# A fixed emission order and ordering edges for the expert stage of a one-core hybrid encoder layer

## The chip, the cores and the metric

One core of one Trainium2 chip runs the whole layer. The metric is the device time of one execution in microseconds (us); before the change the median of three runs is 1244.87 us.

## What is computed

One layer over 1024 tokens of width 1024: a combined projection, differential attention and a state-space mixer, an output projection with LayerNorm that gives `h`, and a mixture of 32 experts on `h`, with a closing LayerNorm. The change touches the experts alone. The reference picks one of four groups for each token and two of its eight experts, and then computes, for each expert `e` and the tokens that chose it:

```python
def block_fn(args):
    tok, w, e = args
    xb = h2d[tok]
    hid = jax.nn.silu(xb @ w_gate[e]) * (xb @ w_up[e])
    yb = hid @ w_down[e]
    return yb * w[:, None].astype(yb.dtype)
```

`w_gate` and `w_up` are 1024 x 512 and `w_down` is 512 x 1024 per expert, all in float32. A first block of 128 places per expert is worked off in straight code; tokens beyond 128 of one expert go to a loop at the end, which these inputs leave empty.

## The kernel before

Attention, the mixer, the output projection and the routing come first and are not changed. The experts start about 540 us into the span and end near 1190 us; a tail adds the two results of each token and normalizes.

**Weights.** Each expert has six pieces of 1 MB: two halves each of gate (`g0`, `g1`), up (`u0`, `u1`) and down (`d0`, `d1`). SyncE's queue (SP) loads a piece into a ring of 12 buffers (`load_next`, L1169 and L1173; three more buffers at the start). `split_next` then writes it as a high and a low part, so that three fast matmul passes stand for a full-precision one: ScalarE (ACT) rounds to the high part (`split`, L172), VectorE (DVE) subtracts for the low part (L153), each in two instructions a piece. There are three pairs of split buffers (`NSPL = 3`): the split of piece n+3 writes where piece n was, and so waits for the product of piece n.

**Products.** `product` issues 12 matmuls of 128x512 for a piece (L1235 for gate and up, L1226 for down). The list `order` names the pieces: `g0 u0 g1 u1` of expert e, then `d0 d1` of expert e-1.

**Turning.** `tokens(e)` transposes the 128 gathered rows of an expert (eight matmuls against the identity into `xT`, L1199) and splits them into `xe`. `hidden(e)` applies silu to the gate sum (ACT, L1205, into `hd`, which the trace calls `gx`), multiplies by the up sum (DVE, L156), transposes that (four matmuls into `hT`, L1209) and splits it into `he`. `result(e)` scales the down sum (ACT, `yo`, L1242), adds the residual (DVE, L162), scatters the rows and gathers those of expert e+5 (POOL, L1139 and L1134).

**Overflow table.** Where piece 63, the second down half of expert 9, is to be loaded, `overflow_blocks` first uses its buffer for 25 small DVE instructions on the routing (tiles `over`, `place`, `blk`, `meta`), with one matmul (`counts`). The load of that piece waits for the last reader of that buffer. SP, like the other engines, also reads `meta` into a register for the loop at the end (L1340), and that read stands in SP's queue among the loads.

**What sets the order.** The program's text does not set the order on an engine. The framework traces the program and schedules it at build time by its own estimate of times; whatever is estimated to be ready first is put first. The result is one fixed list per engine, and on the chip each engine works its list off in order.

Of the kernel before, what the change touches and what calls it, by code (L numbers as in the profile page):

```python
# [11 lines left out]
F32 = mybir.dt.float32  # L12
F32R = mybir.dt.float32r
BF16 = mybir.dt.bfloat16
I32 = mybir.dt.int32
AF = mybir.ActivationFunctionType
# [3 lines left out]
P = 128  # L20
D = 1024
# [5 lines left out]
NE = 32  # L27
# [3 lines left out]
EPS = 1e-5  # L31
NSLOT = 25
NONE = 4096
STATS, MULS, ADDS, NGRP = 'VVVVVAVV', 'QQGGGVGQ', 'VVVVVVVV', 1
GB = 0
ASK, GLU, WO = (6, 12), (15, 16, 1, 20, 21, 1), (22, 24, 26, 30)
# [7 lines left out]
NEARSPL = 0  # L44
# [68 lines left out]
def tile_kernel(ctx: ExitStack, tc: tile.TileContext, I: dict, out: bass.AP, dbg=None):  # L113
    nc = tc.nc
    V, S, G, PE, SP = nc.vector, nc.scalar, nc.gpsimd, nc.tensor, nc.sync
# [7 lines left out]
    sl = Slots()  # L123
# [19 lines left out]
    h_dram = dram.tile([T, D], F32, name="h_dram")  # L143
# [11 lines left out]
    def mul(out_, a, b, eng=V):  # L155
        eng.tensor_tensor(out=out_, in0=a, in1=b, op=ALU.mult)  # L156
# [951 lines left out]
    NRAW, NSPL, NXG = 12, 3, 5  # L1108
# [11 lines left out]
    def gx(e):  # L1120
        return gxs[e % NXG // 2][:, e % NXG % 2, :]

    def deep(n):

        if NSPL <= n < NSPL + NLENT:
            return lent[n - NSPL], NRAW + NLENT
        return raw_ring[(n if n < NSPL else n - NLENT) % NRAW], NRAW + (NLENT if n < NRAW + NSPL + NLENT else 0)
# [3 lines left out]
            G.memset(gx(j), 0.0)  # L1131

    def gather(dst, ix):
        G.indirect_dma_start(out=dst, out_offset=None, in_=h_dram[:, :],  # L1134
                             in_offset=bass.IndirectOffsetOnAxis(ap=ix, axis=0),
                             bounds_check=T - 1, oob_is_err=False)

# [20 lines left out]
    def load_next():  # L1158
        n = st_["load"]
        if n == NOVER:  # L1160
            over.extend(overflow_blocks(deep(n)[0]))
        e, m = order[n]
        j = int(m[1])
        slot = deep(n)[0]
        if m[0] == "d":
            r = sl.at(slot, [P, 2, D], F32, f"rw{e}{m}")
            src = w_d[e, 256 * j:256 * j + 256, :].rearrange("(p k) n -> p k n", p=P)
            for ks in (slice(0, 1), slice(1, 2)) if n == len(order) - 1 else (slice(0, 2),):
                SP.dma_start(r[:, ks, :], src[:, ks, :])  # L1169
        else:  # L1170
            r = sl.at(slot, [P, 4, 512], F32, f"rw{e}{m}")
            src = w_g if m[0] == "g" else w_u
            SP.dma_start(r, src[e, 512 * j:512 * j + 512, :].rearrange("(p k) n -> p k n", p=P))  # L1173
        raws[e, m] = r
        st_["load"] += 1

    def split_next():
        n = st_["split"]
        e, m = order[n]
        r = raws.pop((e, m))  # L1180
        a, b = (sl.at(spl_ring[2 * (n % NSPL) + j], list(r.shape), F32R, f"w{'hl'[j]}{e}{m}") for j in range(2))
        if n == len(order) - 1:
            for j in range(2):
                for hs in HALVES:
                    split(a[:, j, hs], b[:, j, hs], r[:, j, hs])
        else:
            n = r.shape[1] // 2
            for j in range(2):
                js = slice(j * n, j * n + n)
                split(a[:, js, :], b[:, js, :], r[:, js, :])  # L1190
        hls[e, m] = (a, b)
        st_["split"] += 1

    def tokens(e):

        g_ = gx(e)
        b_ = bank2(f"xT{e}")
        for kt in range(KT):
            PE.transpose(b_[:, kt * P:(kt + 1) * P], rows(g_, kt), ident)  # L1199
        xT[e] = t_ = xes[e % 2]  # L1200
        split(t_[:, 0], t_[:, 1], b_.rearrange("p (k q) -> p k q", k=KT))

    def hidden(e):
        g_, u_ = acc.pop((e, "g")), acc.pop((e, "u"))
        S.activation(hd[:, 0, :], g_, AF.Silu)  # L1205
        mul(hd[:, 1, :], u_, hd[:, 0, :])
        b_ = bank(f"hT{e}", 1)
        for kt in range(4):
            PE.transpose(b_[:, kt * P:(kt + 1) * P], places(hd[:, 1, :], kt), ident)  # L1209
        t_ = hes[e % 2]  # L1210
        split(t_[:, 0], t_[:, 1], b_.rearrange("p (k q) -> p k q", k=4))
        hid[e] = t_

    def product(e, m):
        a, b = hls.pop((e, m))
        j = int(m[1])
        if m[0] == "d":
            if j == 0:
                acc[e, "y"] = bank2(f"y{e}")
            y = acc[e, "y"]  # L1220
            for k in range(2):
                kt = 2 * j + k
                passes = list(enumerate(((0, a), (0, b), (1, a))))
                for hs, (n, (x_, w_)) in ([(hs, p_) for hs in HALVES for p_ in passes] if e == NE - 1 else
                                          [(hs, p_) for p_ in passes for hs in HALVES]):
                    PE.matmul(y[:, hs], hid[e][:, x_, kt, :], w_[:, k, hs],  # L1226
                              start=(kt == 0 and n == 0), stop=(kt == 3 and n == 2))
        else:
            if j == 0:
                acc[e, m[0]] = bank(f"{m[0]}{e}")  # L1230
            o = acc[e, m[0]]
            for k in range(4):
                kt = 4 * j + k
                for n, (x_, w_) in enumerate(((0, a), (0, b), (1, a))):
                    PE.matmul(o, xT[e][:, x_, kt, :], w_[:, k, :],  # L1235
                              start=(kt == 0 and n == 0), stop=(kt == KT - 1 and n == 2))
# [14 lines left out]
    def overflow_blocks(key):  # L1251
# [45 lines left out]
        op.close()  # L1297
        return meta, place, blk

    for e in (0, 1, 4):  # L1300
        gather(gx(e), idx[:, 0, e:e + 1])
    tokens(0)
    for n, (e, m) in enumerate(order):
        while st_["split"] < min(len(order), n + NSPL):
            while st_["load"] < min(len(order), st_["split"] + deep(st_["load"])[1]):
                load_next()
            k = st_["split"]
            with ExitStack() as late_:
                if k < NSPL:
                    late_.enter_context(tc.issue_after((normed if k < NEARSPL else routed).ins))  # L1310
                    if k > 0:
                        late_.enter_context(tc.issue_after(turned.ins))
                split_next()
        if n == NLENT:
            he_all = sl.at(lent[0], [P, 2, 2, 4, P], F32R, "he")
            hes = [he_all[:, j] for j in range(2)]
            gxs[1] = sl.at(lent[1], [P, 2, D], F32, "gx1")
            yos = sl.at(lent[2], [P, 2, D], F32, "yo")
            for j in (2, 3):
                G.memset(gx(j), 0.0)  # L1320
                gather(gx(j), idx[:, 0, j:j + 1])
        product(e, m)
        if m == "u1":
            hidden(e)
        if m == "g1" and e + 1 < NE:
            tokens(e + 1)
        if m == "d1":
            result(e)
    meta, place, blk = over
    sl.back([deep(n)[0] for n in range(len(order) - NRAW, len(order))])  # L1330

# [149 lines left out]
```

## Time and profile before

| | |
|---|---|
| runs | 1244.34, 1244.87, 1251.14 us (median 1244.87) |
| profiled execution | 1243.16 us, of which the span of the trace is 1241.4 us |
| PE (matmul) busy | 1101.2 us (89%) |
| DVE busy | 970.2 us (78%) |
| ACT busy | 703.2 us (57%) |
| DMA bytes, mean rate | 271.01 MB, 218 GB/s |
| mean granted clock of TensorE | 0.934 |

The span runs from the first to the last instruction; the 1.8 us around it belong to the execution and not to any engine. A share is a mean over stages with different limits, and the stage in question is about half of the span. PE's clock has two levels, 1.2 and 2.4 GHz; the profile gives it as a share of the higher (0.5 and 1.00).

### The profile page before, as it was taken

What the parts mean: (1) busy time and instruction counts of PE and PEld (TensorE: products, weight loads), DVE (VectorE), ACT (ScalarE), POOL (GpSimd) and SP (SyncE); (2) the same over time, 40 slices, a digit from 0 to 9 for tenths busy, and PEclk for the clock granted to TensorE, in tenths of its full rate; (3) what the DMA queues carried; (4) which work ended last, traced back from release to release, by engine and by line L of the source; (5) the groups of instructions that cost most, each with busy time, mean ns of one, the idle gap of its engine ahead of it and who ended that gap; (6) DMA issues with size and microseconds to landing.
All of it is one profiled execution on the core that took longest, in us unless ns stands there. A gap on an engine that the chain in (4) does not pass through costs nothing. (4 is left out here: it accounts for less than half of the span.)

```text
span 1241.4 us, 15031 instructions
## 1 busy us (share of the span) xinstructions
PE 1101.2 (89%) x5313; PEld 909.2 (73%) x5313; DVE 970.2 (78%) x1409; ACT 703.2 (57%) x941; POOL 386.1 (31%) x279
## 2 busy tenths in 40 slices
PE   7988999889899999969999998899999997899910
PEld 5876777767688788857888886688888875688710
DVE  5598677657777664476999998699999987699947
ACT  3222433445765632226888885587888866588702
POOL 0068464322543541442136522110113110223024
PEclk9988999988899899968999999899999998899965
DMA  5631121211201562655999999699999997789166
GB/s 192 153 86 49 40 57 26 56 35 34 68 1 34 175 234 100 243 184 193 336 370 394 370 350 366 235 373 381 369 364 381 377 343 293 271 320 383 72 233 190
DMA packets 89213, 271.01 MB, mean 218 GB/s; under 512 B 30128, under 2 KB 50608, under 8 KB 64688
## 3 DMA queue, kind: packets, MB, share of 16 engines
q1 hardware_dynamic: 65968, 245.18, 53.5%
q0 software_dynamic: 11216, 23.61, 6.3%
q10 hardware_dynamic: 11952, 1.23, 0.7%
q8 instruction: 43, 0.70, 0.2%
q14 instruction: 34, 0.28, 0.1%
HBM read 254.12 MB, written 27.26 MB: 227 GB/s over the span
## 5 line engine op out<-in xcount | busy, mean ns | idle before, releaser
L1139 POOL DMA_INDIRECT moe_dram<-yo,idx x32 | 70.1, 2192 | 253.3 <-DVE yo L162 220.8
L1134 POOL DMA_INDIRECT gx<-h_dram,idx x32 | 74.0, 2314 | 233.8 <-issue 74.4
L231 PE MATMUL proj<-xh,wa 128*128 128x512 f32 x256 | 76.0, 403 | 1.6 <-ACT ssm L672 1.6
L231 PE MATMUL proj<-xh,wb 128*128 128x512 f32 x256 | 75.9, 409 | 1.6 <-ACT ssm L672 1.6
L1069 PE MATMUL mix<-woh,mx 128*128 128x512 f32 x256 | 73.7, 398 | 0.0
L784 ACT ACTIVATE p<-s,nm 128x1024 f32<-128x1024 f32 (+7 forms) x64 | 47.2, 742 | 26.3 <-DVE nm L797 19.7
L172 ACT CAST xe<-xT 128x1024 fp32r<-128x1024 f32 x32 | 32.4, 1012 | 47.2 <-PE xT L1199 22.4
L231 PEld LDWEIGHTS proj<-xh,wb 128*128 128x128 f32 x256 | 50.0, 198 | 12.3 <-ACT ssm L672 1.8
L231 PEld LDWEIGHTS proj<-xh,wa 128*128 128x128 f32 x256 | 48.9, 194 | 11.3 <-ACT ssm L672 1.8
L1069 PEld LDWEIGHTS mix<-woh,mx 128*128 128x128 f32 x256 | 47.5, 190 | 9.4 <-DVE mx L153 0.3
L779 PE MATMUL s<-kk,qh 128*128 128x512 f32 (+3 forms) x96 | 42.2, 439 | 11.2 <-ACT p L784 10.3
L1199 PE MATMUL xT<-ident,gx 128*128 128x128 f32 x256 | 39.4, 296 | 13.4 <-DMA gx<-h_dram,idx 6.7
L153 DVE TENSOR_TENSOR xe<-xT,xe 128x1024 fp32r<-128x1024 f32 x32 | 39.0, 1219 | 15.2 <-ACT xe L172 14.7
L1199 PEld LDWEIGHTS xT<-ident,gx 128*128 128x128 f32 x256 | 37.8, 207 | 17.5 <-ACT yo L1242 7.8
L162 DVE SCALAR_TENSOR_TENSOR yo<-gx,first,yo 128x1024 f32<-128x1024 f32 (+1 forms) x33 | 41.1, 1247 | 12.1 <-ACT yo L1242 12.1
L1242 ACT ACTIVATE yo<-y,WT 128x1024 f32<-128x1024 f32 (+1 forms) x33 | 35.9, 1091 | 21.9 <-PE y L1226 21.9
L797 DVE TENSOR_REDUCE nm<-s 128x1 f32<-128x1024 f32 (+3 forms) x32 | 32.5, 1019 | 14.6 <-PE s L781 14.6
L817 PE MATMUL po<-vv,half 128*128 128x128 f32 x288 | 42.9, 290 | 0.0
L231 PE MATMUL proj<-xl,wa 128*128 128x512 f32 x128 | 42.8, 405 | 0.0
L231 PE MATMUL proj<-xl,wb 128*128 128x512 f32 x128 | 42.6, 408 | 0.0
L1069 PE MATMUL mix<-wol,mx 128*128 128x512 f32 x128 | 42.1, 397 | 0.0
L817 PEld LDWEIGHTS po<-vv,half 128*128 128x128 f32 x288 | 37.2, 198 | 1.7 <-ACT half L814 0.3
(862 smaller groups left out, 3541.2 us busy)
## 6 DMA issues: line engine op xcount, KB each, us to landing
misc<-in_w_in_dram SPq DMA_DIRECT2D x16, 512.0 KB, 4.1
mo<-moe_dram SPq DMA_DIRECT2D x11, 512.0 KB, 8.1
xr<-in_x_dram SPq DMA_DIRECT2D x8, 512.0 KB, 6.8
wo_raw<-in_w_out_dram SPq DMA_DIRECT2D x4, 1024.0 KB, 4.8
xa<-in_x_dram SPq DMA_DIRECT2D x8, 512.0 KB, 4.0
h_dram<-xa SPq DMA_DIRECT2D x8, 512.0 KB, 4.2
out_dram<-mo SPq DMA_DIRECT2D x8, 512.0 KB, 2.9
mo<-moe_dram POOLq DMA_DIRECT2D x5, 512.0 KB, 12.4
```

The costliest lines, as they stand in the source:

```text
L153: eng.tensor_tensor(out=out_, in0=a, in1=b, op=ALU.subtract)
L162: return V.scalar_tensor_tensor(out=out_, in0=a, scalar=s, in1=b, op0=op0, op1=op1)
L231: PE.matmul(o[:, hs], wt[kt // 4][:, w_, kt % 4, :], x_[:, hs], start=(kt == 0 and n == 0), stop=(kt == KT - 1 and n == 2))
L779: PE.matmul(s_[:, c0:c0 + w], qd[0][:, c, tk], kk[h][:, c, c0:c0 + w], start=True, stop=False)
L784: S.activation(p_[:, c, 0:n], s_[:, 0:n], AF.Exp, bias=nm[:, c:c + 1], accum_out=L[:, j, c:c + 1])
L797: V.tensor_reduce(out=nm[:, c:c + 1], in_=s_[:, 0:n], axis=AX.X, op=ALU.max, negate=True)
L817: PE.matmul(po[:, j * P:(j + 1) * P], aT[:, k, :], vv[k // 4][:, k % 4, h * P:(h + 1) * P], start=(k == 0), stop=(k == i))
L1069: PE.matmul(o[-(hs.start > 0)][:, hs], mx[:, m_, kt, :], (woh, wol)[w_][kt // 2][:, kt % 2, hs], start=(kt == 0 and n == 0), stop=(kt == K ...
L1134: G.indirect_dma_start(out=dst, out_offset=None, in_=h_dram[:, :], in_offset=bass.IndirectOffsetOnAxis(ap=ix, axis=0), bounds_check=T - 1, ...
L1139: G.indirect_dma_start(out=moe_dram[:, :], out_offset=bass.IndirectOffsetOnAxis(ap=ix, axis=0), in_=src, in_offset=None, bounds_check=2 * ...
L1199: PE.transpose(b_[:, kt * P:(kt + 1) * P], rows(g_, kt), ident)
L1242: S.mul(yo[:, hs], y[:, hs], WT[:, e:e + 1])
```

## The change

The stage is written out in a fixed order, and `keep_order` then adds, from the first gather on, an edge from each instruction to the one before it on the same engine (PE, ACT, DVE, POOL and SP), so that the scheduler can't move them against each other. The edges carry no semaphore. `hidden` is cut in three: `gate` follows the product `g1`, `gated` the product `u1`, and `turn_hidden(e+1)` stands between `d0` and `d1` of expert e. `tokens(e+1)` stands between `u1` of expert e and the next down product; before, the text had it after `g1`, and the transposes of expert 1 could run before the products of expert 0. One split follows each product.

```diff
-    def hidden(e):
-        g_, u_ = acc.pop((e, "g")), acc.pop((e, "u"))
-        S.activation(hd[:, 0, :], g_, AF.Silu)
-        mul(hd[:, 1, :], u_, hd[:, 0, :])
+    def gate(e):
+        S.activation(hd[:, 0, :], acc.pop((e, "g")), AF.Silu)
+
+    def gated(e):
+        mul(hd[:, 1, :], acc.pop((e, "u")), hd[:, 0, :])
+
+    def turn_hidden(e):
         b_ = bank(f"hT{e}", 1)
...
+    def keep_order():
+
+        traced, prev = nc.cur_bb.bb.instructions, {}
+        at = next(k for k, i in enumerate(traced) if i is pins[0])
+        for i in traced[at:]:
+            if i.engine not in ORDERED:
+                continue
+            if i.engine in prev:
+                tc.add_manual_dep(i, prev[i.engine].name,
+                                  mybir.DependencyInfo(mybir.DependencyClass.NoSync, mybir.DependencyReason.DATA),
+                                  reason="keep_order")
+            prev[i.engine] = i
...
+    hes = yos = None
+    refill()
     for e in (0, 1, 4):
-        gather(gx(e), idx[:, 0, e:e + 1])
-    tokens(0)
+        g_ = gather(gx(e), idx[:, 0, e:e + 1])
+        if e == 0:
+            pins = [g_.ins]
+    with tc.issue_after(routed.ins), tc.issue_after(turned.ins):
+        split_next()
+        split_next()
+        tokens(0)
+        split_next()
     for n, (e, m) in enumerate(order):
-        while st_["split"] < min(len(order), n + NSPL):
...
+        refill()
         if n == NLENT:
...
+            borrow()
         product(e, m)
+        if m == "g1":
+            gate(e)
         if m == "u1":
-            hidden(e)
-        if m == "g1" and e + 1 < NE:
-            tokens(e + 1)
+            gated(e)
         if m == "d1":
             result(e)
+        if m == "u1" and e == 0:
+            turn_hidden(0)
+        if st_["split"] < len(order):
+            split_next()
+        if m == "u1" and e + 1 < NE:
+            tokens(e + 1)
+        if m == "d0" and e + 1 < NE:
+            turn_hidden(e + 1)
+    keep_order()
```

`refill` holds the old loop over `load_next`, `borrow` the old lines that lend three buffers. The instructions are the same in number and size, but for their order. Line numbers move by 2 in helpers and by 2 to 35 further down.

**PE, from expert 24 to 25.** In these rows `g`, `u` and `y` are the sums of gate, up and down, and `wh`/`wl` the parts of a split weight, with the expert's number. Before:

```order
L1235 MATMUL g_8056<-wl24g_8051,xe_4368 128x512
L1235 MATMUL g_8056<-wh24g_8050,xe_4368 128x512
L1209 MATMUL hT_8143<-ident,gx_4367 128x128 x4
L1199 MATMUL xT_8110<-ident,gx_4366 128x128 x8
L1235 MATMUL g_8207<-wh25g_8152,xe_4369 128x512
L1235 MATMUL g_8207<-wl25g_8153,xe_4369 128x512
L1226 MATMUL y_8158<-wh23d_8092,he 128x512 x2
```

The change:

```order
L1240 MATMUL u_8079<-wl24u_8072,xe_4368 128x512
L1240 MATMUL u_8079<-wh24u_8071,xe_4368 128x512
L1201 MATMUL xT_8140<-ident,gx_4366 128x128 x8
L1231 MATMUL y_8153<-wh23d_8092,he 128x512 x2
L1231 MATMUL y_8153<-wl23d_8093,he 128x512 x2
L1231 MATMUL y_8153<-wh23d_8092,he 128x512 x4
L1231 MATMUL y_8153<-wl23d_8093,he 128x512 x2
L1231 MATMUL y_8153<-wh23d_8092,he 128x512 x2
L1214 MATMUL hT_8172<-ident,gx_4367 128x128 x4
L1231 MATMUL y_8153<-wh23d_8113,he 128x512 x2
```

The two groups of transposes stood together behind the last product of expert 24, with the first of expert 25 right behind them; now a down product of 12 matmuls stands between them and another behind them, in every expert from 1 on.

**DVE, the overflow table.** Before, its instructions stand singly or in twos among the splits (the first rows):

```order
L166 TENSOR_SCALAR over<-iof 128x7
L1266 MEMSET over 128x32
L153 TENSOR_TENSOR wl9g_5737<-rw9g_5422,wh9g_5736 128x1024
L153 TENSOR_TENSOR wl9u_5758<-rw9u_5450,wh9u_5757 128x1024 x2
L1262 TENSOR_TENSOR over<-counts,over 128x224
L1286 TENSOR_TENSOR over<-rk,over 128x112
L162 SCALAR_TENSOR_TENSOR yo<-gx_4515,first,yo 128x1024
```

In the change all 25 stand together; here the last of them and what is behind:

```order
L164 SCALAR_TENSOR_TENSOR place<-over,rk 128x16
L161 TENSOR_TENSOR blk<-over 128x16
L164 SCALAR_TENSOR_TENSOR blk<-over,blk 128x16
L168 TENSOR_SCALAR blk<-blk 128x16
L158 TENSOR_TENSOR gx_4367<-u_5632,gx_4367 128x512
L155 TENSOR_TENSOR wl9g_5719<-rw9g_5402,wh9g_5718 128x1024 x2
L155 TENSOR_TENSOR xe_4369<-xT_5724,xe_4369 128x1024
```

The product that `hT` of expert 8 needs (`gx` from `u`) and the splits of expert 9 are now behind the whole table. On SP the load of piece 63 moves up, from behind the loads of expert 11 and the first of 13 to its place in the list, with the read of `meta` just ahead of it.

**ACT, from expert 0 to 1.** Only the change is shown (`rw` is a loaded piece):

```order
L174 CAST wh1g_4479<-rw1g_4381 128x1024 x2
L1206 ACT_TABLE_LOAD
L1206 ACTIVATE gx_4367<-g_4447 128x512
L174 CAST wh1u_4498<-rw1u_4383 128x1024 x2
L174 CAST he<-hT_4528 128x512
L174 CAST wh1g_4535<-rw1g_4385 128x1024 x2
L174 CAST xe_4369<-xT_4541 128x1024
```

Before, the cast of `xe` for expert 1 stood ahead of all of these; now it is behind the `he` of expert 0 and one more split.

## Rows read from the trace of the kernel before

**Rows 1.** Windows of the stage: stretch, length, busy us, granted clock, DMA share, GB/s.

```profile
600.00:740.00 140.00, 140.00 (x663) 117.30 (x662) 136.27 (x137) 115.24 (x126) 58.97 (x16) 1.00 0.96 364
740.00:810.00 70.00, 60.18 (x248) 47.20 (x247) 54.47 (x62) 43.33 (x48) 12.17 (x6) 0.90 0.81 314
1000.00:1105.00 105.00, 90.77 (x387) 72.46 (x386) 79.75 (x74) 70.39 (x76) 10.74 (x11) 0.92 0.80 298
```

**Rows 2.** Timeline, PE: first gate matmul of some experts, and the last matmul.

```profile
577.60 0.50 PE L1235 MATMUL g<-wh1g,xe 128*128 128x512 f32 x1 [1.29 <-ACT gx L1205]
595.97 0.48 PE L1235 MATMUL g<-wh2g,xe 128*128 128x512 f32 x1
720.67 0.39 PE L1235 MATMUL g<-wh9g,xe 128*128 128x512 f32 x1
809.61 0.39 PE L1235 MATMUL g<-wh13g,xe 128*128 128x512 f32 x1
1006.58 0.39 PE L1235 MATMUL g<-wh24g,xe 128*128 128x512 f32 x1
1104.94 0.39 PE L1235 MATMUL g<-wh28g,xe 128*128 128x512 f32 x1
1183.35 0.39 PE L1226 MATMUL y<-wh31d,he 128*128 128x512 f32 x1
```

**Rows 3.** Timeline, PE: a group of transposes; 24 matmuls from third row to fourth.

```profile
659.46 1.11 PE L1199 MATMUL xT<-ident,gx 128*128 128x128 f32 x8
660.33 0.48 PE L1235 MATMUL u<-wl5u,xe 128*128 128x512 f32 x1
...
1013.43 0.39 PE L1235 MATMUL u<-wh24u,xe 128*128 128x512 f32 x1
...
1018.88 0.39 PE L1235 MATMUL g<-wh24g,xe 128*128 128x512 f32 x1
```

**Rows 4.** Timeline, DVE: two gated products a period apart; two pieces split in between.

```profile
663.23 0.69 DVE L156 TENSOR_TENSOR gx<-u,gx 128x512 f32<-128x512 f32 x1 [0.45 <-PE u L1235]
...
675.99 4.62 DVE L153 TENSOR_TENSOR wl5d<-rw5d,wh5d 128x1024 fp32r<-128x1024 f32 x4
681.04 0.69 DVE L156 TENSOR_TENSOR gx<-u,gx 128x512 f32<-128x512 f32 x1 [0.43 <-PE u L1235]
```

**Rows 5.** DMA issues between 600 and 740 us: pieces, KB each, median us to landing.

```profile
rw5d<-in_w_exp_down_dram SPq DMA_DIRECT2D x2, 1024.0 KB, 10.2
```

**Rows 6.** Timeline, SP, DVE, PE: down pieces of expert 9.

```profile
714.03 0.33 SPq L1169 DMA_DIRECT2D rw9d<-in_w_exp_down_dram  x1
761.50 0.33 SPq L1169 DMA_DIRECT2D rw9d<-in_w_exp_down_dram  x1
761.32 0.16 DVE L1279 CAST meta<-over 128x16 int32<-128x16 f32 x1
771.36 1.22 PE L1226 MATMUL y<-wh9d,he 128*128 128x512 f32 x2 [3.03 <-ACT wh9d L172]
```

**Rows 7.** Window of the tile `over` alone: DVE busy, instructions, clock, DMA.

```profile
719.00:762.00 43.00, 5.68 (x24) 1.00 0.89 336
```

**Rows 8.** Timeline, PE, from expert 24 to 25.

```profile
1023.17 0.74 PE L1209 MATMUL hT<-ident,gx 128*128 128x128 f32 x4 [1.41 <-DVE gx L156]
1027.71 1.98 PE L1199 MATMUL xT<-ident,gx 128*128 128x128 f32 x8 [3.80 <-ACT yo L1242]
1030.80 0.80 PE L1235 MATMUL g<-wh25g,xe 128*128 128x512 f32 x1 [1.10 <-ACT xe L172]
1033.93 1.20 PE L1226 MATMUL y<-wh23d,he 128*128 128x512 f32 x4
```

**Rows 9.** Timeline, ACT, from expert 0 to 1.

```profile
570.91 2.01 ACT L172 CAST wh1g<-rw1g 128x1024 fp32r<-128x1024 f32 x2 [0.26 <-PE u L1235]
...
575.65 1.28 ACT L1205 ACT_TABLE_LOAD   x1
576.95 0.60 ACT L1205 ACTIVATE gx<-g 128x512 f32<-128x512 f32 x1
```

More of the change, by code (lines that the diff above doesn't have):

```diff
@@ L33 @@
 NONE = 4096
+ORDERED = (mybir.EngineType.PE, mybir.EngineType.Activation, mybir.EngineType.DVE, mybir.EngineType.Pool,
+           mybir.EngineType.SP)
 STATS, MULS, ADDS, NGRP = 'VVVVVAVV', 'QQGGGVGQ', 'VVVVVVVV', 1
@@ L1133, in gather @@
     def gather(dst, ix):
-        G.indirect_dma_start(out=dst, out_offset=None, in_=h_dram[:, :],
+        return G.indirect_dma_start(out=dst, out_offset=None, in_=h_dram[:, :],
                              in_offset=bass.IndirectOffsetOnAxis(ap=ix, axis=0),
@@ L1298, in overflow_blocks @@
         return meta, place, blk
-    for e in (0, 1, 4):
-        gather(gx(e), idx[:, 0, e:e + 1])
-    tokens(0)
-    for n, (e, m) in enumerate(order):
-        while st_["split"] < min(len(order), n + NSPL):
[L1305 to L1313, printed above, removed]
-        if n == NLENT:
[L1315 to L1321, printed above, removed]
+    def keep_order():
[9 more added lines that the diff above has]
+            prev[i.engine] = i
@@ new lines, in refill, with borrow @@
+    def refill():
+        while st_["load"] < min(len(order), st_["split"] + deep(st_["load"])[1]):
+            load_next()
+    def borrow():
+        nonlocal hes, yos
+        he_all = sl.at(lent[0], [P, 2, 2, 4, P], F32R, "he")
+        hes = [he_all[:, j] for j in range(2)]
+        gxs[1] = sl.at(lent[1], [P, 2, D], F32, "gx1")
+        yos = sl.at(lent[2], [P, 2, D], F32, "yo")
+        for j in (2, 3):
+            G.memset(gx(j), 0.0)
+            gather(gx(j), idx[:, 0, j:j + 1])
+    hes = yos = None
```

## The prediction

> **What bounds the kernel now.** Read the stage in windows first [rows 1]. From 600 to 740 us PE is busy for 140.00 of 140 us at full clock, DVE for 136.27, and the DMA share is 0.96: the stage is as good as full, and PE ends it. From 740 to 810 and from 1000 to 1105 PE loses 9.8 and 14.2 us of busy time, its clock falls to 0.90 and 0.92, and the DMA share to 0.81 and 0.80. So the time to win is not in any instruction but in these two stretches. The timeline of PE then gives a clock for the stage, the start of each expert's first gate product [rows 2]. From expert 2 to expert 9 there are 124.70 us in 7 periods, 17.81 us each. Against that period, experts 9 to 13 take 88.94 us where four periods are 71.24: 17.7 lost. Experts 13 to 24 take 196.97 against 195.91: 1.1 lost. Experts 24 to 28 take 98.36 against 71.24: 27.1 lost.
>
> What a period is made of: 24 matmuls take 5.45 us, so a product of 12 takes 2.72, six of them 16.3, and a group of eight transposes 0.87 [rows 3]. With four more transposes, half of that, PE needs some 17.6 of the 17.81. DVE runs its list between two gated products 17.81 apart with one wait of 0.43 to 0.45, so its own work is 17.38 per expert [rows 4]. Both are near the limit; DVE has 0.43 to spare. Loads are not: a piece lands 10.2 us after its issue in this stretch [rows 5], and it is issued when the piece 12 places ahead of it in the ring has been split, two periods or 35 us ahead.
>
> Where the two stretches come from is read in the waits. **First stretch:** the second down piece of expert 9 is issued 47 us behind the first, at 761.50, 0.2 us behind the instruction that writes `meta`; and PE, which has waited 3.03 us for ACT's rounding of it, goes on at 771.36 at half clock (two matmuls in 1.22 us; 0.45 at full clock) [rows 6]. The table instructions that hold this piece back are only 5.7 us of work, spread over 42 us between the splits [rows 7]. **Second stretch:** behind the last product of expert 24 PE has `hT` and then `xT`, and nothing else. It waits 1.41 us for the gated product, then 3.80 us for ACT, which has several casts ahead of `yo`, then 1.10 us for the split of what it has just turned; its first gate matmul then takes 0.80 instead of 0.39, and it is at full clock again some 3 us later [rows 8]. Experts 25 to 27 go the same way.
>
> **The change, part by part.** The sum runs from expert 2's first gate matmul, 595.97, to the last matmul, 1183.35: 587.4 us. The stages ahead of the experts and the tail behind them have the same lists, and are taken as unchanged.
>
> *The period.* In the new list a product of 2.72 us, or more, covers each group of transposes. `hT` follows `u1` by `xT` and `d0`, 0.87 + 2.72 = 3.6 us, in which DVE has to end the split it is in and the gated product of 0.69. `xT` has `d0`, `hT` and `d1` behind it, 5.9 us, before the next gate product wants its split. Is DVE's fixed list slower? Its tightest round goes from the end of `g1` to the end of `g1` one expert on: silu 0.6 and the first half of a cast 1.0 on ACT [rows 9], then on DVE all of its list but two splits, 17.38 less 4.6 [rows 4], and the product 2.72 on PE: 17.1 us, and with an estimated 0.2 for the hand-overs between engines 17.3, below 17.81. So PE keeps ending the period, and I take 17.81 as measured. The bound below is 17.57 (transposes at their own price), 7 us less in 29 periods. The bound above is DVE's 17.38 with two waits of 0.45 instead of one, 18.28, or 14 us more. Whichever holds, 29 periods from expert 2 to 31 and 23 us behind (four products of expert 31, two of 30, two of 31, 8 x 2.72 = 21.8, with `hT` 0.4 and one short wait) are 516.5 + 23 = 539.5. The 47.9 us above that go.
>
> *The start.* Expert 0's four products end about 576.3 as before (1.29 us ahead of expert 1 at 577.60 [rows 2]). Before, the rows of expert 1 had been turned and split by then. Now they stand behind `he` of expert 0 and a split. Walk the list from 572.9, when ACT ends a cast, with the durations of rows 9: table load 1.28, silu 0.60, cast 2.01 (576.8); on DVE the rest of that split (578.2), then the gated product 0.69 (578.9); `hT` (579.6). `xe` is the size of half a piece, so 1.0 on ACT and 1.2 on DVE, and `he` half of that: `he` and a cast on ACT (582.2), `xe` on ACT (583.2) and on DVE behind a split (584.9). Expert 1 starts at 584.9 instead of 577.6: 7.3 us late, with PE standing still twice. I add 1.2 net for a half clock that lasts some 3 us behind such a pause [rows 8], together 8.5; bounds 5 (DVE and ACT catch up sooner) and 12.
>
> *The table.* Its 25 instructions now stand in one piece ahead of the gated product of expert 8: 6 us on an engine with 0.43 to spare, which holds back `hT`, on which PE waits some 5 us, and behind it the splits of expert 9. With 2.5 for half clock I take 8.5; bounds 3 (the three split buffers cover half) and 16 (nearly what the stretch loses now). The load of piece 63 and what stands behind it on SP waits those 6 us too. Between 35 us of lead and 10.2 of landing that is covered; if the lead were gone, each us would be PE's.
>
> *Edges, `refill`, POOL.* The edges add no instruction and no wait. POOL's gather for expert e+5 stays behind the scatter of e, four experts ahead of its use. Both cost nothing while PE ends the period.
>
> Sum: -47.9 + 8.5 + 8.5 = -30.9. Against the profiled execution's 1243.16 us that is 1212.3; its own time is 1.7 below the median of the runs shown, which is inside their spread. **Forecast 1212 us.**
>
> **The rivals.**
> *DVE ends the period.* The fixed list lets DVE wait twice, as bounded above: 18.28 per expert, 1212 + 14 = 1226. For it: only 0.43 to spare. Against it: the round of 17.3.
>
> *A third of it.* The two stretches shrink only by a third (16 us), with the start and the table as above: 1243 - 16 + 17 = 1244. For it: nothing definite; what ends a wait can hide a second cause, as where the profile names an engine and it was a DMA.
>
> *The change doesn't touch the cause.* If the two stretches were the loads' (DMA share 0.96 in the full one), both would stay and the new costs come on top: 1243 + 17 = 1260. Against it: 10.2 us to landing, and a DMA share that is lowest where PE waits [rows 1].
>
> *PE stands before `hT` in every expert.* The list now holds PE there however late DVE is. If DVE is over 3.6 us behind the end of `u1`, PE waits, its clock halves, and each expert looks like 24 to 28 do now, 24.6 us instead of 17.81: 29 x 6.8 = 197 more, about 1409. It decides from 1.1 us per expert on (30.9 / 29). Against it: in the full stretch DVE waits for the up sum and not the other way round [rows 4].
>
> *The clock falls at each group of transposes.* Now they stand as whole groups in all experts, at two places. If each group left the next product at half clock, 2 x 2.72 us per expert, 29 experts would take 158 us more, about 1370. Against it: between 659.46 and 660.33 PE did eight transposes in a row, and the granted clock was 1.00 in that whole window [rows 1, 3]. The Trainium skill, "TensorE: Matmul & The Clock Gate", Part 4: PE-mode transpose, says that transposes don't count as busy for the clock in the way that other matmuls do. By that rule this rival would be the forecast; the trace does not agree with it for groups as short as these.
>
> **How the numbers follow.** Chances: the forecast (1203 to 1222) 0.72, DVE 0.15, a third 0.04, cause untouched 0.04, `hT` 0.03, transposes 0.02. What a measurement of this kernel can tell from no change is about 0.5%, 6 us. Faster by more than that are the first two, 0.87; within it the third, 0.04; slower the other three, 0.09. The range: below, 17.57 per period and the start and table near their lower bounds, 1212 - 7 - 4 = 1201, rounded to 1200; above, DVE's 1226 with 6 more for the table, 1232. It leaves out some 0.15.
>
> **What would show it.** Right: in the profile of the changed kernel the first gate matmuls of experts 13 to 31 are 17.6 to 17.9 us apart with no wait over 1 us on PE and a granted clock of 1.00; expert 1 starts near 585; one wait of some 5 us before `hT` of expert 8; the last matmul near 1152. Wrong: a wait before each `hT` or `xT`; casts of ACT that start only when a piece lands; a period over 18.3; or a clock below 1.00 from 810 us on.

## The result, and the profile after the change

The changed kernel takes 1209.9 us (median of four runs, 1209.22 to 1210.44) against 1245.01 before (1244.34 to 1251.14): a ratio of 0.9713, 95% interval 0.9682 to 0.9744. The forecast was 1212, with 1200 to 1232 as range.

| | before | after |
|---|---|---|
| profiled execution, us | 1243.16 | 1210.23 |
| span, us | 1241.4 | 1208.3 |
| PE busy, us | 1101.2 | 1085.0 |
| DVE busy, us | 970.2 | 971.7 |
| start of the DVE instruction that writes the experts' indices (`idx`), us | 553.64 | 550.64 |
| from there to the last matmul, us | 629.7 | 598.8 |
| mean granted clock | 0.934 | 0.939 |

Work on DVE and ACT is the same; PE's busy time is lower because fewer matmuls ran at half clock. The stretch of the profiled execution that the change touches, from `idx` to the last matmul, is 30.9 us shorter; 3.0 us more come from ahead of it and 0.8 are lost behind it (33.1 of span).

Windows of after (stretch, length, busy us of PE, PEld, DVE, ACT, POOL, clock, DMA share, GB/s), against [rows 1]:

```profile
600.00:720.00 120.00, 120.00 (x566) 100.43 (x565) 116.49 (x108) 99.32 (x109) 25.95 (x14) 1.00 0.97 371
720.00:760.00 40.00, 34.95 (x153) 28.79 (x153) 38.02 (x55) 26.83 (x29) 7.41 (x4) 0.91 0.84 322
760.00:1000.00 240.00, 240.00 (x1135) 201.50 (x1134) 233.04 (x217) 199.13 (x216) 48.21 (x26) 1.00 0.98 382
1000.00:1150.00 150.00, 149.03 (x696) 124.14 (x694) 141.72 (x133) 119.80 (x133) 24.66 (x14) 1.00 0.79 309
```

The late stretch is gone: PE is busy for all of 760 to 1000 us and at full clock to its last matmul. What is left of the first one lies between 720 and 760, behind the wait ahead of `hT` of expert 8 (below).

Timeline of PE, after: first gate matmuls and the last matmul, as in [rows 2], with the longest waits in brackets:

```profile
575.65 0.74 PE L1214 MATMUL hT<-ident,gx 128*128 128x128 f32 x4 [3.23 <-DVE gx L158]
579.87 0.79 PE L1240 MATMUL g<-wh1g,xe 128*128 128x512 f32 x1 [1.88 <-ACT xe L174]
601.44 0.39 PE L1240 MATMUL g<-wh2g,xe 128*128 128x512 f32 x1
...
708.42 0.39 PE L1240 MATMUL g<-wh8g,xe 128*128 128x512 f32 x1
728.40 1.13 PE L1214 MATMUL hT<-ident,gx 128*128 128x128 f32 x4 [5.05 <-DVE gx L158]
733.99 0.39 PE L1240 MATMUL g<-wh9g,xe 128*128 128x512 f32 x1
...
805.32 0.39 PE L1240 MATMUL g<-wh13g,xe 128*128 128x512 f32 x1
...
1001.46 0.39 PE L1240 MATMUL g<-wh24g,xe 128*128 128x512 f32 x1
...
1149.42 0.39 PE L1231 MATMUL y<-wh31d,he 128*128 128x512 f32 x1
```

From expert 13 to 24 there are 196.14 us, 17.83 a period, and every period from expert 2 on is 17.82 to 17.85 but one: 25.57 from expert 8 to 9. In the rows of experts 24 and 25 [rows 8] PE now waits for nothing over 0.5 us.

Timeline of DVE, after, from one gated product to the next, against [rows 4]:

```profile
815.25 2.36 DVE L155 TENSOR_TENSOR wl12d<-rw12d,wh12d 128x1024 fp32r<-128x1024 f32 x2 [0.47 <-ACT wh12d L174]
817.53 0.68 DVE L158 TENSOR_TENSOR gx<-u,gx 128x512 f32<-128x512 f32 x1
...
833.09 2.36 DVE L155 TENSOR_TENSOR wl13d<-rw13d,wh13d 128x1024 fp32r<-128x1024 f32 x2 [0.47 <-ACT wh13d L174]
835.37 0.68 DVE L158 TENSOR_TENSOR gx<-u,gx 128x512 f32<-128x512 f32 x1
```

One wait of 0.47 a period is all that DVE has to spare, as before.

The table after the change, against [rows 6, 7]: SP's queue, and the window of the tile `over`:

```profile
717.90 10.04 SPq L1171 DMA_DIRECT2D rw9d<-in_w_exp_down_dram  x2
719.00:762.00 43.00, 6.14 (x24) 0.92 0.84 320
```

Both loads of the down pieces of expert 9 are issued within 10 us instead of 47 apart. Expert 9's down product waits for nothing.

### The profile page after: what moved, and what is told of

The parts are those of the page before. It is cut to its first block, busy times and chain, and to the rows that moved or that the text cites. A ratio compares the mean times of both kernels' runs of the same rounds, so it can differ in the third digit from the quotient of the medians.

```text
span 1208.3 us, 15031 instructions
## 1 busy us (share of the span) xinstructions
PE 1085.0 (90%) x5313; PEld 902.5 (75%) x5313; DVE 971.7 (80%) x1409; ACT 704.4 (58%) x941; POOL 357.2 (30%) x279
## 5 line engine op out<-in xcount | busy, mean ns | idle before, releaser
L1141 POOL DMA_INDIRECT moe_dram<-yo,idx x32 | 54.0, 1688 | 461.9 <-DVE yo L164 456.6
L1136 POOL DMA_INDIRECT gx<-h_dram,idx x32 | 60.3, 1884 | 24.0 <-DVE WT L161 14.6
L1247 ACT ACTIVATE yo<-y,WT 128x1024 f32<-128x1024 f32 (+1 forms) x33 | 36.0, 1093 | 31.3 <-PE y L1231 31.3
L174 ACT CAST xe<-xT 128x1024 fp32r<-128x1024 f32 x32 | 32.1, 1004 | 12.6 <-PE xT L1201 12.6
L174 ACT CAST wb<-misc 128x512 fp32r<-128x512 f32 x16 | 9.7, 622 | 47.9 <-DMA misc<-in_w_in_dram 38.3
```

The lines of the kernel that those rows point to most:

```text
L174: S.copy(hi, raw)
L1136: return G.indirect_dma_start(out=dst, out_offset=None, in_=h_dram[:, :], in_offset=bass.IndirectOffsetOnAxis(ap=ix, axis=0), bounds_check ...
L1141: G.indirect_dma_start(out=moe_dram[:, :], out_offset=bass.IndirectOffsetOnAxis(ap=ix, axis=0), in_=src, in_offset=None, bounds_check=2 * ...
L1247: S.mul(yo[:, hs], y[:, hs], WT[:, e:e + 1])
```

## The experiments

The numbers under "measured" are medians against runs of the kernel before on the same chip (1243.68 to 1245.18 in the four groups), and periods are differences between first gate matmuls as above.

**e1: no edges.**

```diff
-    keep_order()
```

> The new text without the ordering edges: the scheduler may move the instructions again. In its list the rows of expert 1 stand ahead of the first gate product again, the table is spread over DVE's splits and the load of piece 63 is late on SP, and from expert 26 on the two groups of transposes stand next to each other. Theory (what counts is the order that the engines get, and the edges are what keeps it): experts 9 to 13 lose some 15 us again and the experts from 25 on most of their 27, the start is back at 32 us from expert 0 to expert 2; 1230 to 1250 us, and PE waits over 1 us for ACT or DVE at the transposes of the late experts. Rival (the new places in the text are enough): first gate products 17.8 us apart throughout, 1205 to 1215 us.

Measured: 1254.05 us, ratio 1.0071 (1.0048 to 1.0095): just above the theory's 1230 to 1250, and far from the rival. The start is back at 31.9 us, experts 11 to 12 take 30.73, and periods of 21.2, 26.8, 23.9 and 27.3 stand at experts 25, 27, 28 and 29. New was 19.50 in each of the experts 12 to 20, where PE, and with it the period, waits ahead of the gate product for silu on ACT:

```profile
867.74 0.50 PE L1240 MATMUL g<-wh16g,xe 128*128 128x512 f32 x1 [1.38 <-ACT gx L1206]
```

So the new text alone is worth nothing; the gain needs the edges.

**e2: both groups of transposes behind u1.**

```diff
             gated(e)
+            turn_hidden(e)
...
-        if m == "u1" and e == 0:
-            turn_hidden(0)
...
-        if m == "d0" and e + 1 < NE:
-            turn_hidden(e + 1)
```

> All edges kept, but the transposes of the hidden rows stand directly behind the gated product, so that both groups of transposes stand behind u1 with no product between u1 and them. Theory (a product has to lie ahead of the transposes that wait for DVE): PE stands ahead of hT in each expert until DVE has ended its split and the gated product, 1.5 to 3 us, and goes on at half clock for some us; a period of 20 to 24 us in place of 17.83, 1275 to 1400 us, and in the window from 760 to 1000 us PE's granted clock is below 0.95. Rival (the edges and the fixed order alone are what helps, whatever stands between): a period of 17.8 to 18.1 and 1205 to 1220 us.

Measured: 1293.63 us, ratio 1.0393 (1.0363 to 1.0423), within the theory. The periods from expert 2 on are 19.98 or 21.48, but for 29.59 at the table. Timeline of PE in e2, two experts, and the window:

```profile
771.11 0.94 PE L1214 MATMUL hT<-ident,gx 128*128 128x128 f32 x4 [1.90 <-DVE gx L158]
771.84 1.91 PE L1201 MATMUL xT<-ident,gx 128*128 128x128 f32 x8
...
792.59 0.74 PE L1214 MATMUL hT<-ident,gx 128*128 128x128 f32 x4 [1.90 <-DVE gx L158]
793.17 1.12 PE L1201 MATMUL xT<-ident,gx 128*128 128x128 f32 x8
760.00:1000.00 240.00, 217.17 (x984) 179.34 (x983) 205.04 (x188) 172.71 (x188) 44.50 (x24) 0.97 0.91 334
```

In every expert from 2 on but the one at the table PE stands 1.90 us ahead of `hT`, and behind some of these waits its clock halves (the eight transposes take 1.91 instead of 1.12). The theory's clock below 0.95 did not come: it is 0.97. A product ahead of the transposes that wait for DVE is worth 84 us here, with all edges in place.

**e3: the table at the start.**

```diff
-    NOVER = 63
+    NOVER = 16
```

> The change with the overflow table moved from piece 63 to piece 16, that is into the time before the first products, when DVE waits for the gathered rows. Theory (the 25.57 us between the first gate products of experts 8 and 9, 7.7 over the period, are the table's instructions ahead of one gated product): that difference falls to 17.8 and nothing comes in its place, 1201 to 1204 us. Rival A (the table costs the same wherever it stands, for it holds the load behind it): 17.8 between experts 8 and 9 but 5 to 8 us more ahead of expert 3, 1207 to 1212 us. Rival B (the pause has another cause): 25.6 stays and so does 1210 us.

Measured: 1203.22 us, ratio 0.9681 (0.9647 to 0.9714), as the theory has it. Expert 8 to 9 takes 17.81. At the start 1.4 us are lost in turn, 0.85 from expert 0 to 2 and 0.57 ahead of expert 0: the table runs there from 563.5 to 570.4, behind DVE's wait for the rows (which ends at 560.05) and not in it. Window of e3, in place of the second one of after:

```profile
720.00:760.00 40.00, 40.00 (x192) 33.66 (x192) 39.01 (x37) 33.16 (x36) 7.42 (x4) 1.00 1.00 392
```

**e4: rows of expert 1 earlier.**

```diff
-        if m == "u1" and e + 1 < NE:
+        if m == ("u1" if e else "u0") and e + 1 < NE:
             tokens(e + 1)
```

> The change with the rows of expert 1 turned behind the first up product of expert 0, in place of behind the last one; all else kept. Theory (the start loses because the rows of expert 1 are split behind the hidden rows of expert 0 and one more piece on ACT and DVE): from the first gate product of expert 0 to that of expert 2 it falls from 41.9 us to 35 to 38, 1204 to 1207 us. Rival (the wait ahead of hT of expert 0 is what sets it, which stays): 40 to 42 us and 1208 to 1211 us.

Measured: 1207.35 us, ratio 0.9701 (0.9673 to 0.9729). Expert 0 to 2 takes 37.40 instead of 41.95, as the theory has it; the time is 0.35 us above its range, and `idx` came 3.4 us later than after the change. The 3.23 us ahead of `hT` stay.

**e5: e3 and e4 together.**

> The change with both edits of the runs e3 and e4: the table at piece 16 and the rows of expert 1 turned behind the first up product. Theory (the two losses lie at different places and add): 1209.9 less 6.7 of e3 less 2.5 of e4, 1198 to 1202 us, and from the first gate product of expert 0 to that of expert 2 some 38 us. Rival (the table at the start eats what the earlier rows give there): 1202 to 1204 us, and 41 to 43 us from expert 0 to expert 2.

Measured: 1204.95 us, ratio 0.9685 (0.9667 to 0.9704). Neither: from expert 0 to 2 it takes 40.10 us, between the two. With the table in its list DVE works without a pause from 565.22 to the gated product at 583.49, and the wait ahead of `hT` grows from 3.23 to 4.54:

```profile
584.23 1.13 PE L1214 MATMUL hT<-ident,gx 128*128 128x128 f32 x4 [4.54 <-DVE gx L158]
```

From `idx` to the last matmul it is 9.6 us shorter than after the change (6.4 and 5.1 for the two alone), but the stages ahead, which it doesn't touch, ended 5.7 us later in its profile (see the end).

**e6: before, with the table at the start.** The edit of e3, in the kernel before.

> The kernel before, without edges and in its old text, with the table at piece 16 in place of 63. In its list for PE the two groups of transposes stand next to each other, behind the last product of the expert, in experts 12, 13 and 14 and again in 24, 25 and 26. Theory (the loss is what the list does, and comes wherever the two groups stand together): the step of 33 us from expert 11 to 12 is gone, but experts 13 to 15 and 25 to 27 take 23 to 27 us each; the sum of both is within 10 us of before, 1235 to 1255 us. Rival (the first stretch is the table's and the late load's alone): no period over 21 us outside of experts 24 to 28, 1224 to 1230 us.

Measured: 1256.09 us, ratio 1.0100 (1.0080 to 1.0120). The step of 33 from expert 11 to 12 is gone (18.37), but experts 13 to 16 take 26.90, 26.94, 23.83 and 26.84, and 25 to 28 take 29.30, 24.00, 21.56 and 23.59. That is the theory's picture, and its time is 1 us above the range; the rival is out. Moving the table sent the scheduler to another list with two late stretches. What the table alone cost before can't be read from it.

**e7: edges on PE alone.**

```diff
-ORDERED = (mybir.EngineType.PE, mybir.EngineType.Activation, mybir.EngineType.DVE, mybir.EngineType.Pool,
-           mybir.EngineType.SP)
+ORDERED = (mybir.EngineType.PE,
+           )
```

> The change with edges on PE alone: PE's list is that of the change, row for row; on DVE the table is again spread over the splits, on SP the load of piece 63 is again behind those of expert 11 and the first of 13, and ACT's scaling of the down sums falls behind by up to two casts more in experts 19 to 27. Theory (PE's list carries the gain of the late stretch, the other lists that of the table): no period over 19 us from expert 13 on, but experts 9 to 12 lose 15 to 18 us in place of 7.7 at the piece that comes late; 1215 to 1224 us. Rival A (all lists matter in the late stretch too): periods of 20 us and more from expert 19 on, 1230 to 1260 us. Rival B (PE's list alone decides): 1203 to 1211 us.

Measured: 1258.2 us, ratio 1.0111 (1.0093 to 1.0130): the theory fell, rival A holds. PE's list is that of the change, row for row, and yet expert 10 to 11 takes 34.18 and experts 21 to 25 take 22.70, 23.84, 26.04, 27.13 and 24.66. Timeline of e7, PE and SP:

```profile
769.57 0.38 SPq L1171 DMA_DIRECT2D rw9d<-in_w_exp_down_dram  x1
779.48 1.22 PE L1231 MATMUL y<-wh9d,he 128*128 128x512 f32 x2 [13.87 <-ACT wh9d L174]
...
977.85 1.22 PE L1231 MATMUL y<-wh20d,he 128*128 128x512 f32 x2 [3.31 <-DVE xe L155]
```

The first wait is the late load: the second down piece of expert 9 is issued 46 us behind the first (723.56), and PE, whose list has no other product ahead of it, stands for 13.87 (3.03 in [rows 6]). The second kind names DVE's `xe`: from expert 20 to 24 the down sum has to take the sum buffer that the turned rows have just been in.

**e8: hT of expert 0 later.** e5, and

```diff
-        if m == "u1" and e == 0:
+        if m == "u0" and e == 1:
             turn_hidden(0)
```

> The kernel of e5 with the hidden rows of expert 0 turned behind the first up product of expert 1, in place of right behind expert 0's last product (they are not needed before the first down product, which stands behind expert 1). Theory (what is left of the loss at the start is PE's wait of 3.2 us ahead of this group and the half clock behind it): from the first gate product of expert 0 to that of expert 2 it takes 31 to 34 us, 4 to 6 us less than e5, 1193 to 1197 us. Rival (ACT and DVE are behind at the start, and PE then waits for the splits of expert 1 in their place): 37 to 38 us as in e5 and the same time within 1.5 us.

Measured: 1195.8 us, ratio 0.9615 (0.9595 to 0.9635), the fastest of all: 1.2% below the changed kernel (1195.8 / 1209.9, medians of two groups). From expert 0 to 2 it takes 34.79, 5.3 less than e5, a little above the theory's 31 to 34:

```profile
560.51 0.79 PE L1240 MATMUL g<-wh0g,xe 128*128 128x512 f32 x1 [1.12 <-ACT xe L174]
595.30 0.39 PE L1240 MATMUL g<-wh2g,xe 128*128 128x512 f32 x1
```

Not all of the 9.2 us below e5 is this edit's: from `idx` to the last matmul it is 4.7 shorter, and `idx` itself came 5.3 earlier (see the end).

**e9: edges on all engines but ACT.**

```diff
-ORDERED = (mybir.EngineType.PE, mybir.EngineType.Activation, mybir.EngineType.DVE, mybir.EngineType.Pool,
+ORDERED = (mybir.EngineType.PE, mybir.EngineType.DVE, mybir.EngineType.Pool,
```

> The change with edges on all engines but ACT. PE's, DVE's, POOL's and SP's lists are those of the change in the expert stage; on ACT the scaling of the down sum (yo) stands one to three casts later from expert 13 on. The two large sum buffers keep their roles (rows just turned in one, down sums in the other), which in e7 they did not from expert 20 to 24. Theory (a late yo costs nothing as long as the next down sum doesn't need the buffer that the turned rows have just been in): no period over 19 us from expert 9 on, 1208 to 1214 us. Rival (it is ACT's list as such, with yo late, that made e7 slow): periods of 20 us and more from expert 13 on, 1225 us or more.

Measured: 1277.65 us, ratio 1.0266 (1.0238 to 1.0294): the rival, and by more than it said. Experts 14 to 20 take 22.1 to 25.9. Timeline of e9, ACT, DVE and PE around expert 14:

```profile
836.50 1.11 ACT L1247 ACTIVATE yo<-y,WT 128x1024 f32<-128x1024 f32 x1
837.64 1.28 DVE L164 SCALAR_TENSOR_TENSOR yo<-gx,first,yo 128x1024 f32<-128x1024 f32 x1 [7.36 <-ACT yo L1247]
838.85 2.35 DVE L155 TENSOR_TENSOR wl14g<-rw14g,wh14g 128x1024 fp32r<-128x1024 f32 x2
840.12 0.79 PE L1240 MATMUL g<-wl14g,xe 128*128 128x512 f32 x1 [5.32 <-DVE wl14g L155]
```

On ACT `yo` of expert 12 stands three casts later than in the change. DVE's list is fixed and has the residual add next, so DVE stands still for 7.36 us with a split behind it that could have run, and PE stands 5.32 for that split.

This is the plainest comparison of all. In the traces of e9 and of the change, PE, DVE, POOL and SP have the same lists from expert 2 on, row for row, and ACT's differ in nothing but the places of `yo` of experts 12 to 29. From expert 13 to 31 the period is 21.10 us in the mean against 17.83: a 1.1 us scaling, one to three casts late, costs 59 of the 68 us.

**e10: before, with fixed sum buffers.**

```diff
+    pair = [bank2(f"pair{j}") for j in range(2)]
...
-        b_ = bank2(f"xT{e}")
+        b_ = pair[0]
...
-                acc[e, "y"] = bank2(f"y{e}")
+                acc[e, "y"] = pair[1]
```

> The kernel before, in its old text and without edges, but with the two large sum buffers given out once: turned rows always go to the first, down sums always to the second. Before, the scheduler gave them out as they came free, and the periods of the late stretch, from expert 24 to 28, are those in whose products the down sum takes the buffer that the turned rows have just been in, or the other way round. Theory (that exchange is the late stretch): no period over 20 us from expert 20 on, the first stretch at experts 9 to 13 stays with its 15 to 18 us, 1210 to 1225 us. Rival (the scheduler's list is slow in itself, whatever buffers it uses): late periods of 21 us and more remain, 1235 to 1255 us.

Measured: 1269.23 us, ratio 1.0187 (1.0150 to 1.0225): the theory fell, and the time is above the rival's range too. Experts 23 to 26 take 26.97, 26.89, 23.55 and 23.45, now with waits ahead of the gate product:

```profile
1049.12 0.79 PE L1235 MATMUL g<-wh25g,xe 128*128 128x512 f32 x1 [2.58 <-ACT gx L1205]
```

**e11: e10 with the table at the start.**

> The kernel of e10 with the table at piece 16 as well: both stretches treated by their cause, without a single ordering edge. Theory (buffer exchange and table are all that the two stretches are): 15 to 18 us below e10, 1195 to 1208 us. Rival (without edges the scheduler loses as much at another place): 1215 us or more, as in e6 where the table alone was moved.

Measured: 1280.54 us, ratio 1.0290 (1.0264 to 1.0316): the rival. From expert 19 on periods are 20.7 to 23.1, with the same wait of 2.58 for silu in each. The late stretch does not need the exchange of buffers.

**e12: before, with yo held in its place.** What the runs with a slow late stretch share is found on ACT: in each, `yo` falls behind the down sum it scales, two to five experts ahead of the slow periods. The last matmul of the down sum of expert 22 and the `yo` of it, before:

```profile
1012.98 0.62 PE L1226 MATMUL y<-wh22d,he 128*128 128x512 f32 x2
1052.09 1.12 ACT L1242 ACTIVATE yo<-y,WT 128x1024 f32<-128x1024 f32 x1
```

and after the change:

```profile
1001.01 0.61 PE L1231 MATMUL y<-wh22d,he 128*128 128x512 f32 x2
1001.66 1.12 ACT L1247 ACTIVATE yo<-y,WT 128x1024 f32<-128x1024 f32 x1 [0.74 <-PE y L1231]
```

From the end of the sum that is 38.5 us against 0.04. Before, it is at most 1.03 from expert 9 to 18, then 2.4, 13.4, 32.1, 38.5, 32.9, 13.9, 8.7 and 2.4 for experts 19 to 26; in e7 10.6 to 38.9 for experts 18 to 24, in e9, where it holds up DVE directly, 1.9 to 7.4 for experts 12 to 29. At its latest it is 37.6 in e1, 40.8 in e6, 18.5 in e10 and 23.0 in e11. So one kind of edge was added to the text of the kernel before, and nothing else:

```diff
     def split(hi, lo, raw, eng=V):
-        S.copy(hi, raw)
+        c_ = S.copy(hi, raw)
+        if scaled:
+            tc.add_manual_dep(c_.ins, scaled[0].ins.name,
+                              mybir.DependencyInfo(mybir.DependencyClass.NoSync, mybir.DependencyReason.DATA),
+                              reason="yo first")
...
-            S.mul(yo[:, hs], y[:, hs], WT[:, e:e + 1])
+            scaled[:] = [S.mul(yo[:, hs], y[:, hs], WT[:, e:e + 1])]
```

> The kernel before, in its old text, with one kind of edge: on ACT, no cast that the text has after the scaling of a down sum (yo) may be put ahead of it. All else is left to the scheduler, the table at piece 63 and the roles of the sum buffers too. In its list each yo stands where the change has it, behind the casts of u of the expert two on; before, it was up to ten casts later from expert 19 to 26. Theory (in each slow run so far a yo that falls 10 to 40 us behind its sum comes one to four experts ahead of the slow periods; this is the cause of the late stretch): no period over 20 us from expert 14 on, the first stretch stays, 1244 less 27, 1210 to 1224 us. Rival (late yo is only one sign of a list that is bad as a whole): periods of 21 us and more from expert 14 on, 1232 us or more.

Measured: 1219.24 us, ratio 0.9804 (0.9776 to 0.9831): the theory. From expert 24 to 28 it takes 71.45 us instead of 98.36. From expert 14 on one difference is over 20 (21.16, from expert 21 to 22), with no wait over 0.6 us in it: a first matmul moved within the list; the 18 periods from expert 13 to 31 are 17.70 us in the mean (19.25 before). `yo` is never over 1.95 late from expert 8 on. Windows of e12, and its wait for the late piece:

```profile
740.00:810.00 70.00, 58.53 (x252) 46.93 (x251) 55.96 (x64) 44.84 (x49) 18.25 (x6) 0.90 0.83 305
1000.00:1105.00 105.00, 105.00 (x497) 88.10 (x497) 100.97 (x94) 86.39 (x96) 17.91 (x11) 1.00 0.99 387
771.01 1.22 PE L1232 MATMUL y<-wh9d,he 128*128 128x512 f32 x2 [8.27 <-ACT wh9d L174]
```

The late stretch of [rows 1] is gone. The first is there still: 91.05 us from expert 9 to 13, 88.94 before.

One thing limits what e12 shows. The edge acts at build time, and the lists of all engines came out anew with it: of PE's 5313 instructions some 680 stand elsewhere, and from expert 24 to 28 its two groups of transposes no longer stand together. Timeline of PE in e12, with eleven matmuls left out:

```profile
1022.43 1.11 PE L1205 MATMUL xT<-ident,gx 128*128 128x128 f32 x8
...
1025.93 0.63 PE L1215 MATMUL hT<-ident,gx 128*128 128x128 f32 x4
```

So e12 shows that lists in which `yo` is held have no late stretch. It does not tell the lateness of `yo` from the order on PE that comes with it; for `yo` alone e9 speaks.

## Why the prediction was right, and where its reasons were not

**The sum.** From `idx` to the last matmul the forecast was 30.9 us less, and 30.9 were measured. Term by term:

- *The two stretches, -47.9:* from expert 2 to the last matmul, without the table's term, 587.4 became 540.2, so 47.1 went. The period is 17.83 where 17.81 was taken, and 23.2 us stand behind the start of expert 31 where 23 were. The loads, DVE as the new bound, and a third of the gain, the rivals on this term, are out: DMA share 0.98 with PE full, and DVE still waits 0.47.
- *The start, +8.5:* measured from `idx` to expert 2, 42.33 became 50.80, 8.5 more. That the two agree is luck: two errors of 2.0 us cancelled. Expert 1 comes 29.2 us behind `idx` where the walk gave 31.3. The hand-overs were walked well (ACT's part of `xe` ends 29.2 behind `idx`, 29.6 walked), but the walk has PE wait for DVE's part, and the 1.88 us end with ACT's, at 579.82; DVE's ends at 581.49. Timeline of DVE, after:

```profile
580.27 1.22 DVE L155 TENSOR_TENSOR xe<-xT,xe 128x1024 fp32r<-128x1024 f32 x1
```

From the start of expert 1 to that of expert 2 it takes 21.57 where 18.37, as before, and 1.2 for the clock were taken. Behind the waits of 3.23 and 1.88 PE is at half clock until some 586; by the two windows below that costs an estimated 3.4 us. Windows of after, from the first gate matmul of expert 1:

```profile
579.90:584.00 4.10, 3.65 (x8) 2.44 (x9) 1.59 (x2) 0.00 (x0) 0.00 (x0) 0.50 0.66 210
584.00:590.00 6.00, 6.00 (x23) 4.82 (x22) 2.36 (x2) 2.76 (x3) 0.00 (x0) 0.78 0.09 34
```

- *The table, +8.5:* 7.74 (25.57 against 17.83), with the one wait of 5.05 ahead of `hT` of expert 8. e3 shows that all of it is the table's place.

**A reason that was not enough.** The second stretch was put down to PE's list: `hT`, then `xT`, "and nothing else", and the gain to the products that now cover them. Uncovered groups do cost by themselves: in e2, with all lists fixed and no `yo` late, the period is 2.7 us longer. But covering them is not enough: with exactly PE's new list and the other engines free, periods of 22.70 to 27.13 come back (e7), and with nothing changed but `yo` on ACT 18.0 to 25.9 (e9). What the prediction left out is ACT's list. It had the clue in hand, "3.80 us for ACT, which has several casts ahead of `yo`" [rows 8]: the step from that wait back to ACT's list, and to how long ago that sum had been ready, was not taken. That the uncovered groups on PE are themselves what a late `yo` leads to is argued and not shown: the scheduler writes both lists at once, and in e12 both went together. Why its estimate puts `yo` back there stays open.

The Trainium skill says in "Perfetto Trace Analysis", section "Optimization Strategy", that a gap which repeats over a stretch can mean too few buffers for the next tile. Here the late stretch looked like that, PE waiting for a sum buffer; but e12 has the same buffers and no gap, and e10, which gave them out otherwise, kept it.

**Smaller readings.** "Experts 25 to 27 go the same way" holds in part: ahead of expert 26 PE waits 1.65, 1.69 and 1.10 us, ahead of expert 27 1.21 and 1.77, the last for DVE's `xe` and not for `yo`. The lower bound of a period, 17.57, is a little under what its rows give (three times 5.45 and one and a half times 0.87 are 17.65). In [rows 6] the 0.45 set beside 1.22 is the step from one pair to the next; a pair at full clock is listed with 0.62, and 1.22 is half clock all the same. The 10.2 us to landing [rows 5] are the longest median of the stretch, not a common one (4.7 to 10.2), which is on the safe side.

**The edges.** That they add "no instruction and no wait" is right with all engines tied: 1209.9. With some tied and others not, edges made it slower than none: 1258.2 (PE alone) and 1277.65 (all but ACT), against 1254.05 without. A fixed list is only as good as the arrival of what it waits for, and each engine's list sets that for the others.

**The rivals that ended slower.** PE standing ahead of `hT` did not come, since `u1` is followed by `xT` and a product. Its price was too high: 24.6 us a period was taken from [rows 8], and e2, which makes it happen, has 20.5 in the mean: it has one wait of 1.90 where [rows 8] has three (1.41, 3.80 and 1.10), and the clock halves behind some of them alone. The clock did not fall at the transposes: from 760 to 1000 us each expert has its twelve of them in two whole groups, and the granted clock is 1.00. The Trainium skill, "TensorE: Matmul & The Clock Gate", Part 4: PE-mode transpose, says they don't count as busy in the same way; this trace does not show a cost of that between products.

**The time in all.** 1212.3 was summed for the profiled execution, and it took 1210.23: the difference is the 3.0 us that the stages ahead were shorter, less 0.8 of the tail, neither foreseen.

## What to carry to other kernels

Where an engine waits for a buffer or a result, go back to the list of the engine that frees it and measure how long ago that instruction could have run; before, a 1.1 us scaling stood back by up to 38.5 us, and holding this one kind of instruction in place, with the new lists that came of it, gave 25 us of the 35. Here it paid to tie all the lists that feed each other, or the one instruction that drifts, and not a part of the engines. In a fixed list keep a product ahead of each transpose that waits for another engine, and put rare work (the table, the first hidden rows) where that engine has time: the two, with the rows of expert 1 earlier, gave 14 us more in e8.

## What the runs showed of the hardware

The stages ahead of the experts end at different times though no edit touches them: `idx` came between 549.69 us (e6) and 557.82 (e7). Much of it arises in a few microseconds of the attention, where the granted clock differs. Windows of before and of e6:

```profile
282.00:294.00 12.00, 12.00 (x56) 9.93 (x55) 7.32 (x13) 7.54 (x16) 1.43 (x3) 0.66 0.20 43
...
282.00:294.00 12.00, 12.00 (x80) 10.20 (x80) 9.77 (x15) 9.06 (x22) 5.33 (x4) 1.00 0.21 44
```

It was 0.54 in e5 and 0.96 in e3 and after the change. A profile shows one execution of each kernel, so that this belongs to the kernel and not to the execution is not shown; but the times speak for it. The traces of e5 and e8 have the same lists as far as `idx`, reach it at 556.33 and 551.00 and differ by 4.7 us from there on; their medians lie 9.2 apart, and the four executions of either within 2.6. So of the 33 us of the profiled execution 3 are not shown to be the change's.

And the same wait does not always cost the same: in e2 PE stands 1.90 us in each expert, but 10 of the 28 periods from expert 2 on, the table's apart, are 1.5 us longer, those in which the clock halves behind the wait. The twelve transposes stand directly behind each of these waits, and what part they have in it is not separated; but in e11, where the wait is 2.58 us and a gate product stands behind it, the granted clock of the next 3 us is 1.00 in 8 of the 13 experts from 19 on and 0.50 to 0.73 in the other 5.
